# Modulation scales and shifts summed along the free axis, and a first feed-forward part that begins by pairs of feature tiles

## The chip, the cores and the metric

The kernel runs on one core of one Trainium2 chip. The core has a matrix engine (TensorE), a vector engine (VectorE), an activation engine (ScalarE), a general engine (GpSimd) and a queue engine (SyncE), each with a queue of its own that it works off in order, and transfers that are issued from SyncE's and ScalarE's queues. The metric is the time of one execution on the device in microseconds, the median of several runs. In the profile the engines are called PE (products), PEld (the weight loads of products), DVE, ACT, POOL and SP.

## The reference

Two stacks of two layers each work on 256 tokens of 1024 features, one sequence, in f32. The change concerns the first stack. There a vector `c` of 1024 features gives nine vectors of 1024 values for each layer, which scale, shift and gate the three parts of the layer:

```python
cond = jax.nn.silu(c)
for l in range(DEPTH):                                   # 2 layers
    mod = cond @ ada_w[l] + ada_b[l]                     # 1024 x 9216
    sh1, sc1, g1, sh2, sc2, g2, sh3, sc3, g3 = jnp.split(mod, N_MOD, axis=-1)

    hn = _modulate(_rms_norm(h, norm_g[l, 0]), sh1, sc1)             # xn * (1 + sc) + sh
    h = h + 0.5 * g1[:, None, :] * _swiglu(hn, ffn1_w_in[l], ffn1_w_out[l])   # 1024 -> 2 x 2816 -> 1024

    hn = _modulate(_rms_norm(h, norm_g[l, 1]), sh2, sc2)
    ...                                                  # mixing: differential and forgetting attention,
    h = h + g2[:, None, :] * (mixed @ w_out[l])          # a causal convolution, a gated spatial mixing

    hn = _modulate(_rms_norm(h, norm_g[l, 2]), sh3, sc3)
    h = h + 0.5 * g3[:, None, :] * _swiglu(hn, ffn2_w_in[l], ffn2_w_out[l])
```

The second stack follows (three kinds of attention with gates, and an MLP of 4096), without modulation.

## The kernel before

All activations stay in SBUF: `h[0]` and `h[1]` hold the residual stream of the two token tiles of 128. Weights come as units of at most 128 x 1024 f32 (0.52 MB) in one long `stream`, in the order in which they are used; `fetch` issues a transfer from SyncE's queue as long as at most 8 units are raw. A unit is converted by `pump` into a high part (a cast on ScalarE to a rounded format) and a low part (a subtraction on VectorE), and then is a chunk; units marked "whole" skip this. Each product of a chunk is made of three matmuls: high by high, high by low, low by high. All tiles of 4 KB a partition come from one ring, the arena (40 places, `c` in the profile); banks of PSUM are `bank`, small results `st`, scratch `ev`.

The order of all instructions is written out when the program is traced. `Plan` keeps an estimate of the time at which each engine ends what it was given. The main stream is the products of TensorE (`gemm_in`, `gemm_out`). Between its products `tick` calls `pump`, and moves on background generators (`Background`): the urgent ones, then the first four others, each when the plan says that its inputs are ready. `wait` and `drain` do the same until a condition holds. `pump` holds a chunk's conversion back where VectorE or ScalarE is late by the plan; units of the modulation are not held back so.

Modulation: the nine vectors of a layer are in `ada_w` as eight units each, with 128 input features as partitions and 1024 output features along the row. The first scale and shift (`v` = 1 and 0 of layer 0) come by halves of the output features, four units of 2 x 512 for each half (`first_half`). The scale of these goes through TensorE, as products with one row of output (`ada_unit`, `v == 1`), and is turned into columns by 128x1 products (`ada_turn`). All other vectors are summed on VectorE: a multiply by `cond[:, kt]` for the first unit and a multiply-add for each other. The sums over the partitions come after: for scales and shifts by 8 transposes on TensorE and 2 reductions on VectorE (`ada_columns`, `ada_reduce`), for gates (`v % 3 == 2`) by a product with ones.

`Normed` makes the input of a part: squares and their sum on ScalarE, a power on GpSimd, rows scaled by it, and `to_xT`, which transposes four feature tiles at a time into a bank, applies scale and shift by feature tile on the way out (on ScalarE for the first half of the features, on VectorE for the second) and splits the result into high and low. In the first feed-forward part of layer 0 (`st["want"] == 0`) three blocks of weights (`EARLY`) run at once, each for the first half of the features, tile 0 and tile 1, and then for the second half. The stream there is: eight half units of modulation (x's tile 0 after the fourth), the chunks for the first half of the features of three blocks (x's tile 1 among them, after the twelfth fetch), the other eight half units, and the other six chunks. The remaining 54 units of the part (part 0) follow, with the 48 units of six further vectors of layer 0 spread among the units from 4 to 50. Part 1 is the mixing part of layer 0: 24 units of `w_in` (blocks 3 and 5 whole) and 8 units of `w_out` (whole). Its output product goes through the pieces in the order forgetting attention, spatial mixing, convolution, differential attention. Parts 2, 3 and 5 are further feed-forward parts with modulation units among theirs.

Nearly all instructions are issued by one helper (line 183), so the profile's groups are told apart by engine, operation and tile.

Of the kernel before, what the change touches and what calls it, by code (L numbers as in the profile page):

```python
# [70 lines left out]
class Plan:  # L71
    """An estimate of when each engine ends what it was given, in microseconds: it orders the instructions as they are traced."""
# [24 lines left out]
    def put(self, table, ap, stamp):  # L97
        """within one engine the later stamp takes the place of an earlier one"""
# [107 lines left out]
class Background:  # L206
    """Work between the products of the main stream, as generators whose steps follow once what the last one gave
    the other engines is done. The urgent ones all move on with each tick, of the rest the first few."""
# [27 lines left out]
    def idle(self):  # L236
        """nothing for the tensor engine to do: on to the next step that is due"""
# [5 lines left out]
def two_blocks(ctx: ExitStack, tc, w, out, dbg=None, stages=99):  # L243
# [9 lines left out]
    X0, X1, EARLY = 4, 12, 3  # L253
    BOTH = 0
    WHOLE = (3, 5)
    FIRST = (0, 0, 0, 0, 0, 0)
# [17 lines left out]
    # banks of PSUM: the products of the main stream keep some to themselves  # L274
# [8 lines left out]
    # the arena: chunks of weights have a part of it to themselves  # L283
# [7 lines left out]
    def ripe(*aps):  # L291
        """the other engines are done with these"""
# [49 lines left out]
    for l in range(L):  # L342
        for i in range(3):
# [4 lines left out]
            else:  # L348
                add(f"ffn{i // 2 + 1}_w_in", l, in_sizes(FFN_BLOCKS), lambda u: u < FIRST[3 * l + i])
# [14 lines left out]
    # the modulation's weights go between those of the feed-forward parts that have time for them  # L364
# [4 lines left out]
    # the first two vectors by halves of the features: the first products begin with the first half of x's  # L369
    def first_half(v, hf):  # L370
        return [(w["ada_w"][0, at * P:(at + 2048) * P].rearrange("(k p n) -> p k n", k=2, p=P)[:, :, 512 * hf:512 * hf + 512], 1024, (0, v, (hf, j)))
                for j in range(4) for at in [(v * KT + 2 * j) * 1024]]
# [19 lines left out]
    st = dict(fetch=0, conv=0, raws=0, held=0, made=0, released=0, want=0, hurry=0, hold=True)  # L392
# [6 lines left out]
    between = {}  # L399

    def fetch():
        while st["fetch"] < len(stream) and st["raws"] < NRAW and spare():
            ap, n = stream[st["fetch"]][:2]
            t = arena.take([P, 1024])
            nc.sync.dma_start(t.rearrange("p (k n) -> p k n", k=2) if len(ap.shape) == 3 else t[:, :n], ap)
# [7 lines left out]
            if st["fetch"] in between:  # L413
                between.pop(st["fetch"])()
# [6 lines left out]
    def pump(force=False, most=None, goal=None):  # L421
        while True:
# [21 lines left out]
            if st["hold"] or st["made"] - st["released"] >= NMOST or not (spare(2) or (force and ahead <= 0 and arena.free >= 2)):  # L444
                return
# [31 lines left out]
    def release(c):  # L477
        """a chunk's last product is out; its place is free with the next tick"""
# [28 lines left out]
    cond = pool.tile([P, KT], F, name="cond")  # L507
    gains = pool.tile([P, 16], F, name="gains")
# [21 lines left out]
    def rpow(src, scale):  # L530
        """(src * scale + eps) ** -0.5"""
# [13 lines left out]
    ada_acc, mod_val, mod_there = {}, {}, {}  # L545

    def ada_unit(raw, l, v, kt):
        key = (l, v)
        gate = v % 3 == 2
        if isinstance(kt, tuple):  # L550
            hf, j = kt
            if j == 0 and v == 1:
                ada_acc[key] = aux()
            elif j == 0 and hf == 0:
                ada_acc[key] = arena.take([P, D])
            a = ada_acc[key]
            for k2 in range(2):
                k, x = 2 * j + k2, raw[:, 512 * k2:512 * k2 + 512]
                c, part = cond[:, k:k + 1], a[:, 512 * hf:512 * hf + 512] if v == 0 else a[0:1]
                if v == 1:  # L560
                    # the tensor engine has nothing else to do
# [1282 lines left out]
```

## Time and profile before

| | us |
|---|---|
| median of 3 runs (1918.46 to 1919.59) | 1918.57 |
| span of the profiled execution | 1916.7 |
| TensorE busy (products) | 1886.5 |
| VectorE busy | 1308.8 |
| ScalarE busy | 966.7 |
| GpSimd busy | 17.8 |

The profile is of one execution; times in it are us from the first instruction. The busy time of TensorE counts a product until a modelled end, so a full TensorE is not one at its peak rate. 396.80 MB are moved, all but 3.4 MB of the program's by SyncE's queue. The granted clock of TensorE is 0.996 of full speed in the mean.

### The profile page before, as it was taken

The numbers are of one execution on the slowest core, as the hardware profiler recorded it, in microseconds if no ns is written. First come the engines' busy times: TensorE is split into PE (matmuls) and PEld (weight loads), VectorE is DVE, ScalarE is ACT, GpSimd is POOL, SyncE is SP. The second block draws the span as 40 slices with busy tenths as digits, with TensorE's granted clock in tenths as the row PEclk, the third lists the DMA queues.
The fourth block names the chain that finished last, engine by engine and source line by source line (L and its number), as shares of the span: only waits on it lengthen the run. The fifth ranks groups of instructions, "written<-read, shape, count | busy, mean of one in ns | idle before, by whom it ended". The sixth has DMA issues, their size and how long they took to land.

```text
span 1916.7 us, 24124 instructions
## 1 busy us (share of the span) xinstructions
PE 1886.5 (98%) x8808; PEld 1498.3 (78%) x8808; DVE 1308.8 (68%) x1995; ACT 966.7 (50%) x1492; POOL 17.8 (1%) x56
## 2 busy tenths in 40 slices
PE   7999999999999999999999999999999999999998
PEld 3888865788888887668888787888888787888886
DVE  5999788777688877865566546666654645666561
ACT  4544456544454535564454646555543645555451
POOL 0000000000000000000000000000000000000000
PEclk9999999999999999999999999999999999999999
DMA  9999763578788876436574353654574443564460
GB/s 374 341 322 371 257 216 114 209 263 283 255 287 284 313 258 208 165 102 204 198 255 169 103 160 107 211 174 156 178 249 143 141 156 100 197 197 159 145 226 33
DMA packets 112483, 396.80 MB, mean 207 GB/s; under 512 B 12262, under 2 KB 12390, under 8 KB 112364
## 3 DMA queue, kind: packets, MB, share of 16 engines
q1 hardware_dynamic: 111068, 391.88, 59.3%
q10 hardware_dynamic: 1296, 3.38, 0.5%
q8 instruction: 69, 1.13, 0.2%
q14 instruction: 50, 0.41, 0.1%
HBM read 394.16 MB, written 1.05 MB: 206 GB/s over the span
## 4 chain that ended last, share of the span: by engine, by line
PE 87%; DVE 6%; ACT 5%; DMA 1%; issue 1%; POOLq 0%; ACTq 0%; POOL 0%; DVEq 0%
PE bank L183 87%; DVE c L183 3%; ACT c L183 2%; DVE sm L183 2%; ACT sm L183 2%; ACT L175 1%; DMA c<-in_ada_w_dram 0%; DVE st L183 0%; DMA c<-in_w_out_b_dram 0%; ACT ev L183 0%; DVE ev L183 0%; DMA col<-in_cols_dram 0%; DVE h L183 0%; ACT st L183 0%; ACT dl L183 0%
## 5 line engine op out<-in xcount | busy, mean ns | idle before, releaser
L183 PE MATMUL bank<-c,c 128*128 128x512 f32 (+3 forms) x7392 | 1763.5, 396 | 8.0 <-ACT c L183 5.8
L183 PEld LDWEIGHTS bank<-c,c 128*128 128x128 f32 (+1 forms) x7392 | 1348.3, 188 | 322.0 <-issue 45.4
L183 DVE TENSOR_TENSOR c<-c,c 128x1024 fp32r<-128x1024 f32 (+3 forms) x604 | 709.3, 1197 | 234.9 <-ACT c L183 227.5
L183 ACT CAST c<-c 128x1024 fp32r<-128x1024 f32 (+1 forms) x590 | 588.7, 1036 | 112.9 <-PE bank L183 77.6
L183 DVE SCALAR_TENSOR_TENSOR c<-c,cond,c 128x1024 f32<-128x1024 f32 (+1 forms) x126 | 153.7, 1220 | 0.8 <-DMA c<-in_ada_w_dram 0.3
L183 ACT ACTIVATE ev<-bank 128x256 f32<-128x256 f32 (+1 forms) x100 | 40.2, 402 | 195.6 <-PE bank L183 195.1
L183 ACT CAST c<-bank 128x512 fp32r<-128x512 f32 (+1 forms) x100 | 55.3, 553 | 92.1 <-PE bank L183 92.1
L183 DVE TENSOR_TENSOR c<-bank,c 128x512 fp32r<-128x512 f32 (+2 forms) x108 | 69.7, 648 | 25.3 <-ACT c L183 25.2
L183 ACT ACTIVATE junk<-h 128x512 f32<-128x512 f32 x44 | 27.8, 631 | 103.4 <-DVE h L183 97.6
L183 ACT ACTIVATE ev<-bank,st 128x512 f32<-128x512 f32 x56 | 38.6, 689 | 77.6 <-PE bank L183 77.6
L183 DVE TENSOR_TENSOR ev<-ev,bank 128x256 f32<-128x256 f32 x88 | 36.7, 417 | 56.8 <-ACT ev L183 56.4
L183 PE MATMUL bank<-con,ev 128*128 128x128 f32 x432 | 72.3, 272 | 2.6 <-DVE ev L183 2.6
L183 PEld LDWEIGHTS bank<-con,ev 128*128 128x128 f32 x432 | 55.7, 139 | 24.0 <-issue 4.3
L183 ACT CAST c<-ev 128x512 fp32r<-128x512 f32 x32 | 19.8, 620 | 99.8 <-DVE ev L183 99.6
L183 ACT ACTIVATE c<-bank,st 128x512 f32<-128x512 f32 x36 | 24.8, 689 | 75.2 <-PE bank L183 69.7
L183 DVE TENSOR_TENSOR ev<-ev 128x512 f32<-128x512 f32 x32 | 22.1, 691 | 45.5 <-ACT ev L183 45.5
L183 DVE TENSOR_TENSOR ev<-bank,c 128x512 f32<-128x512 f32 x40 | 27.4, 685 | 34.7 <-PE bank L183 34.4
L183 DVE SCALAR_TENSOR_TENSOR c<-c,col,c 128x256 f32<-128x256 f32 x120 | 48.7, 476 | 0.0
L183 DVE TENSOR_TENSOR c<-ev,c 128x512 fp32r<-128x512 f32 x32 | 22.2, 692 | 30.8 <-ACT c L183 30.7
L183 DVE TENSOR_TENSOR h<-h,bank 128x512 f32<-128x512 f32 x16 | 10.9, 683 | 42.1 <-PE bank L183 42.1
L183 ACT ACTIVATE sm<-sm,st 128x128 f32<-128x128 f32 x72 | 31.8, 443 | 14.3 <-DVE st L183 14.3
L183 PEld LDWEIGHTS bank<-con,c 128*128 128x128 f32 (+1 forms) x248 | 28.9, 143 | 11.6 <-DVE c L183 3.2
(107 smaller groups left out, 703.7 us busy)
## 6 DMA issues: line engine op xcount, KB each, us to landing
c<-in_ffn_w_in_dram SPq DMA_DIRECT2D x176, 512.0 KB, 5.0
c<-in_w_in_dram SPq DMA_DIRECT2D x152, 512.0 KB, 4.2
c<-in_ada_w_dram SPq DMA_DIRECT2D x144, 512.0 KB, 5.9
c<-in_ffn_w_out_dram SPq DMA_DIRECT2D x88, 512.0 KB, 5.7
c<-in_w_up_dram SPq DMA_DIRECT2D x64, 512.0 KB, 4.3
c<-in_w_down_dram SPq DMA_DIRECT2D x64, 512.0 KB, 4.2
c<-in_w_out_dram SPq DMA_DIRECT2D x16, 512.0 KB, 4.1
c<-in_w_o_dram SPq DMA_DIRECT2D x16, 512.0 KB, 4.5
```

The costliest lines, as they stand in the source:

```text
L175: self.eng.preload_act_table_set(table)
L183: return fn(*args, **kw)
```

## The change

Scales and shifts: their weights lie transposed in memory, 128 output features as partitions and 1024 input features along the row. `cond_row` holds silu(c) in every partition. One VectorE instruction per unit multiplies the unit by `cond_row` and sums along the row into one column of the vector's tile, with `ada_b` as the initial value; after each second unit the pair of columns is finished. The transposes, the reductions, the one-row products and the turning into columns are gone. Gates are as before.

The start: a broadcast of `c` goes out from ScalarE's queue, both tiles of x and the constants are first on SyncE's queue, and both tiles' rows are scaled before the first weights are taken. The stream then comes by pairs of feature tiles: two units of scale and two of shift, then the chunk of that pair for each of three blocks, four times. `Normed` of this part works in four steps of two feature tiles, evicted on ScalarE alone; the first three blocks run pair by pair, tile 0 and then tile 1. A chunk that these blocks ask for is converted alone, not with what else is there.

The other vectors: of the six that lay in part 0, four stay (units 2 to 48), and two, the shift and scale of the third part, go among units 16 to 32 of part 1.

```diff
-    stream = first_half(1, 0) + first_half(0, 0)
-    among = {0: (modulation(0, 2, 4, 3, 5, 7, 6), 4, 50), 2: (modulation(0, 8) + modulation(1, 1, 0, 2), 10, 60),
+    stream = []
+    among = {0: (modulation(0, 2, 4, 3, 5), 2, 48), 1: (modulation(0, 7, 6), 16, 32), 2: (modulation(0, 8) + modulation(1, 1, 0, 2), 10, 60),
              3: (modulation(1, 4, 3, 5, 7, 6), 8, 60), 5: (modulation(1, 8), 12, 56)}
     for part, us in enumerate(parts):
         if part == 0:
-            blocks = [us[4 * b:4 * b + 4] for b in range(EARLY)]
-            stream += [u for b in blocks for u in b[:2]] + first_half(1, 1) + first_half(0, 1) + [u for b in blocks for u in b[2:]]
+            sc0, sh0 = modulation(0, 1), modulation(0, 0)
+            for c in range(4):
+                stream += [u for k in (2 * c, 2 * c + 1) for u in (sc0[k], sh0[k])] + [us[4 * b + c] for b in range(EARLY)]
             us = us[4 * EARLY:]
...
-            pump(force=True)
+            pump(True, goal=i + 1 if i < 4 * EARLY else None)
...
     def ada_unit(raw, l, v, kt):
         key = (l, v)
-        gate = v % 3 == 2
...
+        if v % 3 != 2:
+            t = mod_tile(l, v)
+            ve.tensor_tensor_reduce(raw, raw, cond_row, scale=1.0, scalar=K("ada_b", 72 * l + 8 * v + kt, 1), op0=OP.mult, op1=OP.add,
+                                    accum_out=t[:, kt:kt + 1])
+            if kt % 2:
+                if v % 3 == 1:
+                    a = slice(kt - 1, kt + 1)
+                    ve.scalar_tensor_tensor(t[:, a], t[:, a], 1.0, K("norm_g", 24 * l + 8 * (v // 3) + kt - 1, 2), op0=OP.add, op1=OP.mult)
+                mod_there[key].append(kt // 2)
             return True
...
-        else:
-            for hf in range(2):
-                yield from ada_columns(l, v, hf, acc)
...
-        for hf in range(2):
+        n = KT // steps
+        for step in range(steps):
+            hf = step * 2 // steps
...
-                for j in range(4):
-                    k = 4 * hf + j
-                    if (j % 2 if st["made"] < BOTH else hf):
+                for j in range(n):
+                    k = n * step + j
+                    if steps == 2 and hf:
                         ve.tensor_scalar(x[:, j], ps[:, j], A[:, k:k + 1], B[:, k:k + 1], op0=OP.mult, op1=OP.add)
                     else:
                         sc_.activation(x[:, j], ps[:, j], AF.Identity, scale=A[:, k:k + 1], bias=B[:, k:k + 1])
...
-            order = [(b, tt, part) for part in (whole[:2], whole[2:]) for tt in range(2) for b in range(EARLY)]
+            order = [(b, tt, whole[c:c + 1]) for c in whole for tt in range(2) for b in range(EARLY)]
...
-            norms.append(Normed(mods=((l, 3 * i + 1), (l, 3 * i)), keep=i == 1 or FIRST[3 * l + i] > 0))
+            norms.append(Normed(mods=((l, 3 * i + 1), (l, 3 * i)), keep=i == 1, steps=2 if norms else 4))
...
-    between[X0], between[X1] = lambda: rows_in(0), lambda: rows_in(1)
+    nc.scalar.dma_start(cond_row, w["c"].to_broadcast([P, D]))
+    plan.clock["dma"] = 2.5
+    plan.wrote(cond_row, 5.0, "dma")
+    for tt in range(2):
+        rows_in(tt)
+    sc_.activation(cond_row, cond_row, AF.Silu)
     sc_.activation(cond, K("c"), AF.Silu)
-    for i in range(8):
-        while st["conv"] <= i:
-            pump(True, i + 1)
-        plan.clock["pe"] = max(plan.now, plan.clock["dve"] - 2.0)
-        bg.tick()
...
+    begin(lambda: all(norms[0].rs[tt] is not None for tt in range(2)))
+    pump(True, 4)
+    begin(lambda: all(norms[0].there))
...
-    a["ada_w"] = each("ada_w", lambda t: np.concatenate([lay_out(t[:, v * D:(v + 1) * D]) for v in range(9)]))
+    a["c"] = g["c"].reshape(1, D)
+    a["ada_w"] = each("ada_w", lambda t: np.concatenate([lay_out(m if v % 3 == 2 else m.T) for v in range(9) for m in [t[:, v * D:(v + 1) * D]]]))
```

## Rows read from the trace of the kernel before

**Rows 1.** The page: span's busy times by engine, and tenths in 40 slices.
```profile
PE 1886.5 (98%) x8808; PEld 1498.3 (78%) x8808; DVE 1308.8 (68%) x1995; ACT 966.7 (50%) x1492; POOL 17.8 (1%) x56
...
PE   7999999999999999999999999999999999999998
```
**Rows 2.** Stretches: length, busy us (x) of PE, PEld, DVE, ACT, POOL; PEclk, DMA share, GB/s.
```profile
20.00:30.00 10.00, 7.01 (x23) 5.60 (x24) 7.62 (x10) 8.21 (x14) 0.74 (x2) 0.67 1.03 397
...
80.00:100.00 20.00, 20.00 (x93) 16.36 (x93) 19.81 (x21) 10.15 (x14) 0.00 (x0) 1.00 0.95 324
...
260.00:280.00 20.00, 20.00 (x78) 11.92 (x75) 19.68 (x42) 5.91 (x12) 0.00 (x0) 1.00 0.63 221
280.00:300.00 20.00, 20.00 (x122) 15.37 (x121) 17.98 (x78) 13.79 (x43) 0.00 (x0) 1.00 0.47 161
300.00:320.00 20.00, 18.99 (x91) 11.08 (x90) 16.46 (x68) 15.01 (x44) 0.00 (x0) 1.00 0.32 107
320.00:340.00 20.00, 19.74 (x54) 9.21 (x53) 12.17 (x16) 11.88 (x21) 0.74 (x2) 1.00 0.25 79
```
**Rows 3.** Timeline of the start: start us, us, engine, operation, xcount [idle before <-releaser].
```profile
11.23 0.63 ACT L183 ACTIVATE junk<-h 128x512 f32<-128x512 f32 x1 [5.49 <-DMA h<-in_x_dram]
...
22.99 8.16 PE L183 MATMUL bank<-c,c 128*128 128x512 f32 x27 [3.23 <-ACT c L183]
...
31.09 7.03 PE L183 MATMUL bank<-c,cond 128*1 128x512 f32 x16
...
45.91 12.32 PE L183 MATMUL bank<-c,c 128*128 128x512 f32 x51
```
**Rows 4.** Timeline of TensorE alone, from 64 us.
```profile
64.21 4.38 PE L183 MATMUL bank<-c,c 128*128 128x512 f32 x18
...
68.56 5.74 PE L183 MATMUL bank<-c,c 128*128 128x512 f32 x24
```
**Rows 5.** Timeline of the start: eight transposes of a modulation vector.
```profile
38.05 1.09 PE L183 MATMUL bank<-con,c 128*128 128x128 f32 x8
```
**Rows 6.** Groups by form: xcount, busy us, mean ns of one, idle before, releasers.
```profile
L183 DVE TENSOR_TENSOR c<-c,c 128x1024 fp32r<-128x1024 f32 x574 | 688.4, 1221 | 228.2 <-ACT c L183 221.4 <-PE bank L183 2.2 <-DMA c<-in_ffn_w_in_dram 1.0
L183 ACT CAST c<-c 128x1024 fp32r<-128x1024 f32 x574 | 579.3, 1047 | 104.2 <-PE bank L183 77.6 <-DVE c L183 21.4 <-DMA c<-in_ffn_w_in_dram 2.0
L183 DVE SCALAR_TENSOR_TENSOR c<-c,cond,c 128x1024 f32<-128x1024 f32 x112 | 143.2, 1278 | 0.1
...
L183 DVE TENSOR_TENSOR ev<-ev,bank 128x256 f32<-128x256 f32 x88 | 36.7, 417 | 56.8 <-ACT ev L183 56.4
...
L183 DVE TENSOR_TENSOR c<-ev,c 128x512 fp32r<-128x512 f32 x32 | 22.2, 692 | 30.8 <-ACT c L183 30.7
...
L183 DVE TENSOR_REDUCE mod<-bank 128x4 f32<-128x512 f32 x22 | 15.1, 684 | 5.1 <-PE bank L183 5.1
```
**Rows 7.** Timeline of VectorE: masked minimum with accumulator output, 128 and 256 elements.
```profile
282.31 0.28 DVE L183 CUSTOM_DVE_ANT_0 sm<-bank,con 128x128 f32<-128x128 f32 x1
...
282.51 0.42 DVE L183 CUSTOM_DVE_ANT_0 sm<-bank,con 128x256 f32<-128x256 f32 x1
282.86 0.08 DVE L183 DVE_READ_ACCUMULATOR2_ANT st<- 128x1 f32 x1
```
**Rows 8.** Timelines of VectorE and TensorE in the first mixing part.
```profile
274.63 1.22 DVE L183 TENSOR_TENSOR c<-c,c 128x1024 fp32r<-128x1024 f32 x1
...
281.90 0.48 DVE L183 TENSOR_SCALAR c<-bank,col 128x256 f32<-128x256 f32 x1 [1.88 <-ACT c L183]
...
318.24 5.85 DVE L183 TENSOR_TENSOR c<-c,c 128x1024 fp32r<-128x1024 f32 x5 [1.70 <-ACT c L183]
...
328.64 0.48 DVE L183 SCALAR_TENSOR_TENSOR c<-bank,gains,sm 128x256 f32<-128x256 f32 x1
...
329.17 7.99 PE L183 MATMUL bank<-c,c 128*128 128x512 f32 x18 [0.26 <-DVE c L183]
```
**Rows 9.** Transfers by line: xcount, KB each, median us to landing.
```profile
c<-in_norm_final_dram ACTq DMA_DIRECT2D x1, 512.0 KB, 3.3
```

More of the change, by code (lines that the diff above doesn't have):

```diff
@@ L443, in pump @@
                 continue
-            if st["hold"] or st["made"] - st["released"] >= NMOST or not (spare(2) or (force and ahead <= 0 and arena.free >= 2)):
+            if st["made"] - st["released"] >= NMOST or not (spare(2) or (force and ahead <= 0 and arena.free >= 2)):
                 return
@@ L548, in ada_unit @@
         key = (l, v)
-        gate = v % 3 == 2
[L550 to L560, printed above, removed]
-                    pe.matmul(part, c, x, start=k == 0, stop=k == KT - 1)
-                elif k == 0:
-                    ve.tensor_scalar(part, x, c, None, op0=OP.mult)
-                else:
-                    ve.scalar_tensor_tensor(part, x, c, part, op0=OP.mult, op1=OP.add)
-            if j == 3:
-                bg.add((ada_turn if v == 1 else ada_columns)(l, v, hf, a), urgent=True, due=plan.ready(raw if v == 1 else a))
+        if v % 3 != 2:
[7 more added lines that the diff above has]
+                mod_there[key].append(kt // 2)
             return True
@@ L585, in ada_unit @@
         if kt == KT - 1:
[L586 to L588 removed]
+            ve.tensor_tensor(acc[0:1], acc[0:1], br[0:1], op=OP.add)
+            arena.put()
             bg.add(ada_reduce(l, v, acc), urgent=True, due=plan.ready(acc) + 2.0)
         return True
[L592 to L624 removed]
     def mod_tile(l, v):
@@ L709, in chain @@
                 rows = arena.take([P, D])
-                if st["hold"]:
-                    sc_.activation(rows, h[tt], AF.Copy, scale=self.rs[tt])
-                else:
-                    ve.tensor_scalar(rows, h[tt], self.rs[tt], None, op0=OP.mult)
+                ve.tensor_scalar(rows, h[tt], self.rs[tt], None, op0=OP.mult)
             else:
@@ L716, in chain @@
             yield
-            by = (lambda hf: all(hf in mod_there.get(m, ()) for m in self.mods) and (tt == 0 or st["made"] >= 3),
-                  lambda: [mod_val[m] for m in self.mods]) if self.mods else None
+            by = (lambda pair: all(pair in mod_there.get(m, ()) for m in self.mods), lambda: [mod_val[m] for m in self.mods]) if self.mods else None
             yield from until(lambda: room(3 if self.keep else 2))
@@ L722, in chain @@
                 self.x[tt] = arena.take([P, KT, P])
-            yield from to_xT(rows, self.gain, self.xT[tt], by, self.x[tt], there=self.there[tt], have=lambda hf: self.halves[tt] > hf)
+            yield from to_xT(rows, self.gain, self.xT[tt], by, self.x[tt], there=self.there[tt], have=lambda hf: self.halves[tt] > hf, steps=self.steps)
             if self.mods:
@@ L728, in chain, with finish @@
             st["hurry"] -= 1
-        def finish(self, tt, half):
-            wait(lambda: len(self.there[tt]) > half, "rows")
+        def finish(self, tt, pair):
+            wait(lambda: len(self.there[tt]) > pair * self.steps // 4, "rows")
         def free(self):
@@ L765, in start, with to_xT @@
                 (nc.sync, nc.scalar)[hf].dma_start(out[tt * P:tt * P + P, s], h[tt][:, s])
-    def to_xT(src, A, dst, mods=None, whole=None, there=None, have=lambda hf: True):
+    def to_xT(src, A, dst, mods=None, whole=None, there=None, have=lambda hf: True, steps=2):
         hi, lo = dst
@@ L780, in turn, with modulated @@
                 pe.transpose(banks[-1][:, j], src[:, P * k:P * k + P], ident)
+        def modulated(step):
+            return mods is None or all(mods[0](p) for p in range(4 * step // steps, 4 * (step + 1) // steps))
         yield from turn()
@@ L784, in to_xT @@
         if mods:
-            if not mods[0](0):
+            if steps == 2 and not modulated(0):
                 yield from turn()
-                yield from until(lambda: mods[0](0))
+            yield from until(lambda: modulated(0))
             A, B = mods[1]()
-        for hf in range(2):
+        n = KT // steps
+        for step in range(steps):
+            hf = step * 2 // steps
             if hf == len(banks):
                 yield from turn()
-            yield from until(lambda: (mods is None or mods[0](hf)) and (A is None or whole is not None or evr.has(1)))
-            ps, a = banks[hf], slice(4 * hf, 4 * hf + 4)
+            yield from until(lambda: modulated(step) and (A is None or whole is not None or evr.has(1)))
+            a = slice(n * step, n * step + n)
+            ps = banks[hf][:, a.start - 4 * hf:a.stop - 4 * hf]
             if A is None:
```

123 lines of the change are left out of this document (37 added, 86 removed).

## The prediction

> **What bounds the kernel now.** I read the busy times of the page first: TensorE is busy for 1886.5 of 1916.7 us, VectorE for two thirds, and after the first slice nearly every slice of TensorE shows a 9 [rows 1]. So TensorE is the bound nearly everywhere, and an edit pays where it takes instructions off TensorE or fills a stretch in which TensorE waits. Then I read single stretches in the table of stretches [rows 2]: from 80 to 100 us TensorE is full, with VectorE at 19.81 of 20 beside it, so VectorE is a second bound close behind the first in the first feed-forward part. From 260 to 320 us, in the mixing part, VectorE is at 19.68, 17.98 and 16.46 of 20, and in the next 20 us at 12.17.
>
> The start is the only long wait of TensorE. The timeline of the start [rows 3] shows the first main product at 22.99 us, a run of one-row products for the modulation at 31.09 (7.03 us), and an unbroken run of main products only from 45.91. The first three blocks hold 3 x 4 x 2 x 6 = 144 main products. Eight rows of main products, of which four are shown [rows 3, 4], count 27, 9, 12, 51, 12, 12, 18 and 24: 48 are out by 45.9, 141 by 68.56, and the 144th ends at about 69.3. From 64.21 to 68.56 there are 18 main products and 2 transposes [rows 4]; less 0.2 for the transposes (below) a main product costs 0.23 us. 144 cost 33 us, so the first 69.3 us lose 36.
>
> **The change part by part.** The execution shown spans 1916.7 us; the median of the runs is 1918.57, so 1.9 us lie around the span. I add to the span and put the 1.9 back at the end.
>
> *Transposes removed.* Of the twelve scale and shift vectors all but the first scale were summed over the partitions by 8 transposes each. Eight transposes of that form take 1.09 us from first start to last end [rows 5]; less the tail of the last one that is 0.11 each. Outside the start there are ten such vectors: four in part 0 (32 transposes, 3.5 us) and six of layer 1 (48 transposes, 5.3 us). All lie in feed-forward parts where TensorE is full, so they come off the path: -8.8 us. Two reductions a vector (0.68 us each [rows 6]) come off VectorE.
>
> *The new instruction.* A unit's product with the row of silu(c), and its sum, is now one VectorE instruction with two f32 sources in SBUF and an accumulator output. No row has that form. Nearest are the scaled sum that it replaces, two SBUF sources of the same 128x1024 (1278 ns), the subtraction (1221) [rows 6], and the masked minimum with accumulator output: of two in a row the second starts 0.20 us after the first for 128 elements, and 0.35 us are gone for 256, with the read of the accumulator (0.08) inside that [rows 7]. Carried on to 1024 elements that is 1.15 to 1.25; I take 1.2, the middle. A vector is then 9.6 us, against 0.7 + 7 x 1.2 + 2 x 0.68 + 0.4 of small ones = 10.9 before, so VectorE gains a little on every vector but the first scale, which TensorE did before and which now costs VectorE 9.6.
>
> *The start.* Ahead of all weights now go both halves of x, the constants, and a broadcast of c (0.52 MB) on ScalarE's queue; a broadcast of this shape landed 3.3 us after its issue late in the kernel [rows 9]. Transfers run at 397 GB/s [rows 2], 1.3 us for a unit. The first half of x, after 2.95 MB, was there at 11.23 [rows 3], so a landing is at about 3.8 us plus bytes over rate. In the new order the last of the sixteen modulation units lands at about 41.7 and the last of the twelve early chunks at 45.6. If transfers set the end, a cast, a subtraction and 24 products follow (1.05 + 1.15 + 5.5 [rows 4, 6]): 53.3. But VectorE gets 16 x 1.2 for the modulation, 12 x 1.15 for the low parts, 8 low parts of x of about 0.36 (half of the 0.69 for twice the size [rows 6]), 1.5 for the scaled rows and 1.6 for small ones: 39 us. Its first use is near 13 us, because the squares of x stand behind silu of the broadcast on ScalarE, and the first modulation unit stands behind both scaled rows on VectorE. Without a pause it is done at 52 and TensorE at 57.5; with 1.5 us lost at each of four pairs of feature tiles, to the evictions on ScalarE between a pair's sums and its low part, at 63.5. Bounds 53.3 and 64. I take 61.5, nearer to VectorE's end, because its load alone exceeds that of the transfers. Against 69.3 that is -8 us (-16 to -5).
>
> *Part 0 after the start.* Extras fall from 48 to 32 over 46 weight units. VectorE per unit: 1.15 + 0.7 x 1.2 + 0.4 for the hidden rows (two products of 0.42 and a subtraction of 0.69 for four units [rows 6]) = 2.4 us, against TensorE's 12 x 0.23 = 2.8. VectorE comes out of the start with hardly a chunk of lead and meets six evictions at once there: a stall of 0 to 3 us, I take +1, nearer to none since each unit gives back 0.4. The transfers, 1.7 units of 1.3 us a chunk, stay below 2.8.
>
> *Part 1.* Sixteen units move to the second half of the mixing part's weights, from unit 16 on. Their place in VectorE's queue follows the conversion of the last split chunks (the very last at 274.63 [rows 8]); from there they are taken as fast as they land. That is 16 x 1.2 = 19.2 us in a stretch where VectorE is nearly back to back up to 313 [rows 2], with one wait of 1.88 us [rows 8] and 0.3 elsewhere. Queued behind them are the masks and scalings of the differential attention, and TensorE waits for its last piece: the product at 329.17 starts after 0.26 us of idle time that VectorE ended, whose last scaling began at 328.64 [rows 8]. Upper bound: 19.2 - 2.2 of idle time = 17 us. Lower bound 0: VectorE has 7.8 us free from 320 to 340 [rows 2], and the conversions for part 2 before that, five of them in one run of 5.85 us [rows 8], can go behind. I take the middle, +9. A gain is excluded here, since nothing is removed from this stretch. What hides these units is that slack; without it they cost 17.
>
> Sum: -8 - 3.5 - 5.3 + 1 + 9 = -6.8; span 1909.9, time **1911.8 us**.
>
> **The rivals.** (a) *The slack of part 1 takes the moved units whole.* For: TensorE hardly waits there, 0.26 us in the row. Against: VectorE at 19.68 and 17.98 of 20 just ahead. Then -8 - 8.8 + 1 + 0 to 3 gives 1903 to 1906.
>
> (b) *VectorE's queue in part 1 becomes the bound* (the other side): the differential attention ends 17 us later and TensorE waits ahead of the last output products. With the start at its poor end: -5 - 8.8 + 3 + 17 = +6, 1925. It decides from the point where the moved units cost over 13 us. For: the back-to-back stretch. Against: the room from 320 on [rows 2].
>
> (c) *The start gains nothing*: VectorE's 39 us and its pauses end where the old order did. Then 0 - 8.8 + 1 + 9 gives 1920. This is also the case in which the pairs do not do what they say.
>
> [...]
>
> **How the numbers follow.** Forecast (1907 to 1917) 0.45; (a) 0.17; (b) 0.14; (c) 0.13; (d) 0.06; 0.05 for what I have not seen. A measurement of this kernel can tell about 0.2%, 3.8 us, from no change. Faster by more: (a) and the part of the forecast below 1914.7, 0.39 of its 0.45: 0.56. Within: the rest of the forecast, (c), and some of (b): 0.25. Slower: the rest, 0.19. The range from 1902 to 1925 takes in the forecast, (a), (c) and most of (b).
>
> **What would show it.** Right: the accumulating instruction at 1.2 us; no one-row products; the 144th main product ending near 61; VectorE nearly full from 13 to 55 us; 80 fewer transposes outside the start; and in the first mixing part VectorE back to back for longer, with a wait of TensorE for VectorE of about 9 us ahead of the last output products. [...] What would undo the forecast most easily is the order in which the written-out plan puts the moved units between the steps of the attention, which the trace of before cannot show.

## The result and the profile after

| | before | after |
|---|---|---|
| median of the runs, us | 1918.53 (1918.46 to 1919.59) | 1931.77 (1931.21 to 1934.03) |
| span of the profiled execution, us | 1916.7 | 1929.3 |

The change makes the kernel slower by 13.2 us: the ratio is 1.0068, with a 95% interval from 1.0054 to 1.0082. The forecast was 1911.8, with a range up to 1925.

To see where the time went I numbered the main products, TensorE's instructions of the form 128x512 from `c` tiles. There are 7008 in each trace, so the start of the n-th can be set against that of the n-th before. After stands at -2.1 us at the 144th (end of the first three blocks), -5.0 at the 792nd (end of part 0), +19.4 at the 1100th (part 1 is over) and +12.9 at the last. So the start gave 2.1 us, part 0 2.9, part 1 took 24.4, and the rest gave 6.5.

The page of after, busy times, against [rows 1]:

```profile
PE 1871.3 (97%) x8672; PEld 1491.6 (77%) x8672; DVE 1307.2 (68%) x2055; ACT 969.6 (50%) x1501; POOL 17.0 (1%) x56
```

TensorE is busy for 15.2 us less in a span 12.6 us longer: over the whole span the time is in its waits, which grow by 27.8 us. The table of stretches of after, against [rows 2] (columns as there):

```profile
40.00:60.00 20.00, 16.83 (x60) 12.83 (x59) 15.52 (x26) 11.35 (x19) 0.00 (x0) 0.83 1.03 408
80.00:100.00 20.00, 20.00 (x93) 16.42 (x92) 19.96 (x22) 10.44 (x14) 0.00 (x0) 1.00 0.84 298
260.00:280.00 20.00, 20.00 (x73) 12.43 (x72) 19.93 (x41) 5.91 (x12) 0.00 (x0) 1.00 0.89 318
280.00:300.00 20.00, 14.12 (x73) 12.08 (x71) 19.93 (x54) 7.77 (x26) 0.00 (x0) 0.97 0.99 396
300.00:320.00 20.00, 16.13 (x67) 9.70 (x68) 19.02 (x70) 6.43 (x22) 0.00 (x0) 0.69 0.23 76
```

From 260 to 320 VectorE is now at 19.93, 19.93 and 19.02 of 20 (before 19.68, 17.98 and 16.46), and TensorE falls to 14.12 and 16.13 from 280 on (before 20.00 and 18.99). The timeline of TensorE in part 1 of after, against the one in [rows 8]:

```profile
301.62 1.65 PE L183 MATMUL bank<-c 32*128 32x256 f32 x6 [7.49 <-DVE c L183]
303.19 1.54 PE L183 MATMUL bank<-con,sm 128*128 128x128 f32 x6
...
311.65 1.71 PE L183 MATMUL bank<-sm,c 128*64 128x256 f32 x8 [2.11 <-DVE sm L183]
...
329.45 0.82 PE L183 MATMUL bank<-con,sm 128*128 128x128 f32 x6
...
348.54 7.99 PE L183 MATMUL bank<-c,c 128*128 128x512 f32 x18 [1.20 <-DVE c L183]
```

The last row is the product that the prediction watched (at 329.17 before): it is 19.4 us later, but its own wait is 1.20 us. The large wait, 7.49 us for VectorE, comes 47 us earlier, ahead of the scores. What VectorE does before that, from its timeline of after:

```profile
294.29 1.28 DVE L183 CUSTOM_DVE_ANT_0 c<-c,cond_row,col 128x1024 f32<-128x1024 f32 x1
295.50 0.09 DVE L183 DVE_READ_ACCUMULATOR2_ANT mod<- 128x1 f32 x1
295.50 3.25 DVE L183 SCALAR_TENSOR_TENSOR c<-c,col,c 128x256 f32<-128x256 f32 x8
298.67 1.28 DVE L183 CUSTOM_DVE_ANT_0 c<-c,cond_row,col 128x1024 f32<-128x1024 f32 x1
299.88 0.08 DVE L183 DVE_READ_ACCUMULATOR2_ANT mod<- 128x1 f32 x1
299.88 1.28 DVE L183 CUSTOM_DVE_ANT_0 c<-c,cond_row,col 128x1024 f32<-128x1024 f32 x1
301.08 0.08 DVE L183 DVE_READ_ACCUMULATOR2_ANT mod<- 128x1 f32 x1
301.08 0.48 DVE L183 TENSOR_SCALAR c<-bank,col 128x256 f32<-128x256 f32 x1
```

The scaling at 301.08, which TensorE waits for, stands behind sums at 294.29, 298.67 and 299.88 and a run of convolution taps, without idle time. All sixteen moved sums lie between 248.94 and 302.63. The group of the new instruction by form (xcount, busy us, mean ns):

```profile
L183 DVE CUSTOM_DVE_ANT_0 c<-c,cond_row,col 128x1024 f32<-128x1024 f32 x96 | 121.9, 1279 | 0.0
```

The waits are not the whole of part 1. These rows (columns as in [rows 2]) show part 1 as one stretch, first in before, then in after, and then the three pieces of it in which after has the lower granted clock:

```profile
227.10:357.00 129.90, 126.81 (x578) 87.04 (x578) 100.75 (x262) 77.68 (x175) 2.40 (x9) 1.00 0.45 152
222.10:376.30 154.20, 135.74 (x577) 91.95 (x576) 120.67 (x298) 77.72 (x174) 2.45 (x9) 0.94 0.51 185
247.60:251.00 3.40, 3.14 (x7) 2.48 (x8) 3.40 (x7) 0.77 (x2) 0.00 (x0) 0.50 0.56 224
298.80:309.00 10.20, 7.38 (x32) 5.20 (x34) 10.10 (x34) 0.96 (x2) 0.00 (x0) 0.50 0.21 76
312.50:315.80 3.30, 3.30 (x10) 1.52 (x8) 3.27 (x13) 1.60 (x4) 0.00 (x0) 0.50 0.38 124
```

From the 792nd to the 1100th main product TensorE has 576 instructions in both kernels. In after it is idle for 18.5 us in place of 3.1, and busy for 8.9 us longer. So about 15.4 us of the loss are waits and 8.9 are the same products taking longer. For 13.8 us of its work (3.14 + 7.38 + 3.30) the clock is at 0.50; at that level a product takes about twice as long (the transposes above: 1.54 us against 0.82), so by estimate some 7 of the 8.9 us are the clock.

### The profile page after: what moved, and what is told of

Its sections match the earlier page's. It is cut to its first block, busy times and chain, and to the rows that moved or that the text cites. A ratio compares the mean times of both kernels' runs of the same rounds, so it can differ in the third digit from the quotient of the medians.

```text
span 1929.3 us, 23834 instructions
## 1 busy us (share of the span) xinstructions
PE 1871.3 (97%) x8672; PEld 1491.6 (77%) x8672; DVE 1307.2 (68%) x2055; ACT 969.6 (50%) x1501; POOL 17.0 (1%) x56
## 4 chain that ended last, share of the span: by engine, by line
PE 85%; DVE 7%; ACT 5%; DMA 2%; issue 1%; POOLq 0%; SPq 0%; POOL 0%; DVEq 0%; ACTq 0%
PE bank L183 85%; DVE c L183 5%; ACT c L183 2%; ACT sm L183 2%; DMA c<-in_ffn_w_in_dram 2%; DVE sm L183 1%; ACT L175 1%; DVE st L183 0%; DMA c<-in_w_out_b_dram 0%; ACT ev L183 0%; DVE ev L183 0%; DMA col<-in_cols_dram 0%; DVE h L183 0%; ACT dl L183 0%; ACT st L183 0%
## 5 line engine op out<-in xcount | busy, mean ns | idle before, releaser
L183 PE MATMUL bank<-c,c 128*128 128x512 f32 (+3 forms) x7392 | 1764.4, 397 | 19.7 <-ACT c L183 15.0
L183 DVE CUSTOM_DVE_ANT_0 c<-c,cond_row,col 128x1024 f32<-128x1024 f32 x96 | 121.9, 1279 | 0.0
L183 DVE TENSOR_TENSOR c<-bank,c 128x512 fp32r<-128x512 f32 (+2 forms) x108 | 69.9, 649 | 24.4 <-ACT c L183 24.1
L183 ACT CAST c<-ev 128x512 fp32r<-128x512 f32 (+1 forms) x36 | 20.6, 573 | 91.6 <-DVE ev L183 91.2
L183 DVE SCALAR_TENSOR_TENSOR c<-c,cond,c 128x1024 f32<-128x1024 f32 x42 | 53.8, 1280 | 0.0
L183 DVE TENSOR_TENSOR ev<-ev 128x512 f32<-128x512 f32 x32 | 22.1, 691 | 45.5 <-ACT ev L183 45.5
L183 DVE TENSOR_TENSOR c<-ev,c 128x512 fp32r<-128x512 f32 (+1 forms) x36 | 22.8, 633 | 29.8 <-ACT c L183 29.7
L183 DVE TENSOR_TENSOR h<-h,bank 128x512 f32<-128x512 f32 x16 | 10.9, 683 | 42.1 <-PE bank L183 42.1
```

Source lines behind the costliest of these rows:

```text
L183: return fn(*args, **kw)
```

## The experiments

Theory: the sixteen sums delay the attention because they take VectorE's time in a stretch without slack. Rivals: transfers and ring places of the moved units, or the new start. For each kernel the table gives the median, the ratio to before on the same chip with its 95% interval, and the difference from before (us, from the profiled execution) at the start of a main product. A column less the one before it is a stage: 792nd to 1100th is part 1.

| kernel | us | ratio | 144th | 792nd | 960th | 1020th | 1100th | last |
|---|---|---|---|---|---|---|---|---|
| after | 1931.77 | 1.0068 (1.0054 to 1.0082) | -2.1 | -5.0 | -6.3 | +19.4 | +19.4 | +12.9 |
| e1_all_part0 | 1912.38 | 0.9962 (0.9947 to 0.9976) | -0.2 | -3.5 | -4.9 | -0.3 | -0.2 | -5.1 |
| e2_one_moved | 1922.14 | 1.0010 (1.0000 to 1.0020) | -0.6 | -3.0 | -1.2 | +11.5 | +11.5 | +4.8 |
| e3_no_sums | 1914.30 | 0.9972 (0.9961 to 0.9984) | -2.2 | -5.0 | -2.7 | +1.1 | +1.2 | -3.8 |
| e4_before_moved | 1943.39 | 1.0122 (1.0107 to 1.0137) | +0.9 | -0.7 | -3.4 | +26.0 | +26.1 | +25.9 |
| e5_old_start | 1918.94 | 0.9989 (0.9981 to 0.9998) | +2.8 | +0.1 | -1.3 | +5.3 | +5.3 | +0.5 |
| e7_by_threes | 1913.26 | 0.9963 (0.9950 to 0.9975) | -2.0 | -4.9 | -6.3 | +0.2 | +0.4 | -4.6 |
| e8_half_sums | 1903.91 | 0.9918 (0.9904 to 0.9931) | -9.6 | -13.0 | -14.4 | -9.8 | -9.7 | -14.6 |
| e9_order | 1919.31 | 0.9995 (0.9986 to 1.0004) | 0.0 | +0.1 | +0.6 | +0.6 | +0.6 | +0.6 |
| e10_casts_first | 1905.75 | 0.9926 (0.9911 to 0.9941) | -7.7 | -10.9 | -12.3 | -7.7 | -7.7 | -12.5 |
| e11_hold | 1911.42 | 0.9959 (0.9947 to 0.9972) | -1.9 | -4.9 | -6.3 | -5.0 | -2.1 | -7.1 |
| e13_hold_gmlp | 1908.70 | 0.9947 (0.9934 to 0.9959) | -1.8 | -4.8 | -6.2 | -3.3 | -3.0 | -8.1 |
| e14_casts_hold | 1904.08 | 0.9918 (0.9903 to 0.9932) | -7.6 | -10.8 | -12.1 | -9.2 | -8.9 | -13.9 |
| e15_moved_hold | 1928.39 | 1.0054 (1.0037 to 1.0072) | -2.2 | -5.1 | -7.8 | +14.6 | +14.6 | +8.1 |
| e16_moved_early | 1935.11 | 1.0084 (1.0069 to 1.0099) | -2.2 | -5.1 | +6.4 | +22.1 | +22.1 | +15.7 |

### What the move costs

**All six in part 0**, one line of after:

```diff
-    among = {0: (modulation(0, 2, 4, 3, 5), 2, 48), 1: (modulation(0, 7, 6), 16, 32), ...
+    among = {0: (modulation(0, 2, 4, 3, 5, 7, 6), 4, 50), ...
```

> The changed kernel with all six further vectors of layer 0 in part 0 (units 4 to 50) and none in part 1. Theory A (the sixteen moved units delay the mixing part): the 25.7 us that part 1 loses between its 960th and 1020th main product are gone; part 0 gets 48 units in place of 32 and may lose 0 to 6 us, since VectorE then needs about 2.8 us a unit there, as much as TensorE. Time 1906 to 1912. Theory B (the delay of part 1 comes from the new start, which changes what is in the arena and in the queues ahead of it, and not from the move): part 1 still loses 15 us or more, time 1925 or above.

The kernel becomes faster than before by 8.3 us. Part 1 takes 3.3 us in place of 24.4, so the move is the cause and not the start. And part 0 lost nothing by taking all 48 units: it gives 3.3 us here, against 2.9 with 32. A full VectorE alone is therefore no sign of a bound: from 80 to 100 us, in part 0 of after, it is at 19.96 of 20, as full as in part 1, and TensorE is at 20.00 beside it.

**One vector moved**: `0: (modulation(0, 2, 4, 3, 5, 7), 2, 48), 1: (modulation(0, 6), 16, 32)`.

> The changed kernel with one vector (8 units) in part 1 instead of two; the other is in part 0. If the delay is VectorE's time, unit by unit, it halves: 8 x 1.2 = 9.6 us less up to 2.2 of idle time, at the ratio of the two moved vectors (25.7 us for 16 units) 13 us: time 1917 to 1922. If it is a matter of one wait that is missed (a step of the attention that slips behind a conversion, or the weight of the output that comes late), it stays near 25 us (1930) or vanishes (1907).

Part 1 takes 14.5 us, between 3.3 with none and 24.4 with two: about 10 to 11 us for each vector of 9.6 us of VectorE. It is no single missed wait.

**Transfers without sums**:

```diff
+            if l == 0 and v in (6, 7):
+                gp.tensor_copy(t[:, kt:kt + 1], raw[:, 0:1])
+            else:
                 ve.tensor_tensor_reduce(...)
```

> The changed kernel in which the sixteen moved units are transferred and take their places in the ring as before, but their sums on VectorE are left out (a copy of one column on GpSimd stands for each; the shift and scale of the third part of layer 0 are not computed). Theory A (VectorE's time): the loss of part 1 is gone but for a few us, time 1905 to 1910. Theory C (transfers and places in the arena: 8.4 MB more in the mixing part): the loss stays, 1925 or above.

Part 1 takes 6.2 us, so the sums alone are worth 24.4 - 6.2 = 18.2, and the transfers and places are not the cause of these. Part 1 of e3_no_sums as one stretch:

```profile
222.10:358.10 136.00, 129.10 (x577) 88.29 (x576) 102.06 (x267) 76.97 (x173) 11.41 (x25) 0.99 0.59 209
```

Against after, TensorE is idle for 11.6 us less and busy for 6.6 us less: nearly two thirds of the 18.2 us are waits, the rest is products that take longer. The 6.2 us that stay are 2.9 above e1_all_part0; what the transfers and places have in these was not separated.

**Before, with the two vectors moved**: the same line of the stream in the kernel before.

> The kernel before with only the two vectors moved, in the old form (multiply-add on VectorE, then transposes). Theory A: the placement alone costs 20 to 28 us in part 1, and part 0 gives back 0 to 3 because VectorE is nearly full there: time 1936 to 1946. If the placement is harmless without the new instruction or the new start, 1917 to 1922.

Part 1 takes 26.8 us. The placement alone does the harm, in the old form more than in the new one.

**The two vectors at the beginning of part 1**: `1: (modulation(0, 7, 6), 0, 16)`.

> The changed kernel with its two moved vectors among units 0 to 16 of part 1 instead of 16 to 32. VectorE is idle for 6.4 of the 20 us from 240 to 260 in the kernel before and 0.3 of the next 20. If it is the place (VectorE's back-to-back stretch of the attention) that costs, the sums fit partly into that idle time: loss of part 1 of 10 to 18 us, time 1917 to 1925. If VectorE's work is a fixed total up to the end of the part, whatever its place: 24 us or more, 1930.

The waits of TensorE by what it waited for, from 225 to 355 us (us in total, times, longest):

```profile
PE bank L183 <- ACT c L183: 10.8, 4, 4.6
PE bank L183 <- DVE c L183: 7.4, 7, 1.8
PE bank L183 <- DVE st L183: 2.8, 2, 1.7
```

Part 1 takes 27.2 us. The theory of the place, with 10 to 18 us, falls; the number of the other theory came, 24 us or more (VectorE's work as a fixed total up to the end of the part), with a time above its 1930. Of the 27.2 us, 11.2 (from -5.1 to +6.1 at the 840th product) go right at the beginning of the part, where TensorE waits for casts of its chunks, and the attention still loses 15.7 between the 960th and the 1020th. Neither end of the part has room for two vectors, although VectorE in before is idle for 6.4 us from 240 to 260.

### What part 1 takes even without the move

The kernels with the new sums lose 3.2 to 6.2 us in part 1 although nothing, or no VectorE time, was moved into it. Up to 2 us of that is the clock: e1_all_part0 and e7_by_threes give TensorE the same instructions in the same order up to the 1020th product, but from the 960th on the first loses 4.6 us at a granted clock of 1.00, and the second 6.5, with 6.8 us at 0.50. The timeline of VectorE in e1_all_part0:

```profile
303.59 1.23 DVE L183 TENSOR_TENSOR c<-c,c 128x1024 fp32r<-128x1024 f32 x1 [1.89 <-ACT c L183]
...
311.14 1.23 DVE L183 TENSOR_TENSOR c<-c,c 128x1024 fp32r<-128x1024 f32 x1 [1.40 <-ACT c L183]
...
316.80 1.23 DVE L183 TENSOR_TENSOR c<-c,c 128x1024 fp32r<-128x1024 f32 x1 [1.39 <-ACT c L183]
```

These are conversions for part 2, given out between the steps of the attention; each waits for its cast with the next step behind it. In before the first of them is at 314.06. Two runs ask whether the sums or merely the order brings them.

**Sums in the new form, old start.** The kernel before with the new instruction for all scales and shifts outside the start; the row of `c` is loaded after the start's units:

```diff
+        if not gate:
+            t = mod_tile(l, v)
+            ...
+            ve.tensor_tensor_reduce(raw, raw, cond_row, ...)
+            if kt % 4 == 3:
+                finish_mod(l, v, kt // 4)
+            return True
```

> The kernel before, with its old start and all six vectors in part 0, but every scale and shift outside the start summed by the new instruction: the transposes and reductions alone are gone. If TensorE's transposes cost what the prediction put on them, the kernel is 8.8 us faster than before (3.5 in part 0, 5.3 in layer 1), less what the first mixing part takes back (it took 4.6 us of the 4.9 won before it in the changed kernel with all six vectors in part 0): 4 to 9 us faster than before. If they were hidden: within 1 us of before. Beside the changed kernel with all six vectors in part 0 (8.3 us faster than before): equal to it if the new start is worth nothing, 3 us or more behind it if the new start gains.

The whole is 1.6 us faster, less than expected. By stages: 2.8 us lost at the start (TensorE waits 1.9 us longer there and is at a clock of 0.50 for 10.2 us, in before for 6.8), 2.7 given in part 0, 5.2 taken by part 1 with the same three conversions (307.2, 314.8, 321.4) and 6.8 us at 0.50, 4.8 given after it. So the conversions come with the new sums, whatever the start.

**Another order, no other work**: `0: (modulation(0, 2, 4, 3, 5, 7, 6), 2, 48)` in the kernel before.

> The kernel before, with its 48 modulation units of part 0 placed from unit 2 to 48 instead of 4 to 50: no instruction is added or removed, only the written-out order is another. If the order alone moves the mixing part (the 4.6 us that it took back with all six vectors in part 0 are then such a matter of order), the time differs from before by 1 to 5 us in either direction, and the difference arises in the mixing part. If not, the time is within 1 us of before.

0.6 us in the trace, and no conversion between the steps: a shift of the units alone doesn't bring them.

**Holding them back**, on e1_all_part0:

```diff
+            if not force and st["keep"]:
+                return
             if not force and st["hurry"] and ahead >= 4:
...
         gemm_in(n_, MIX_BLOCKS, evac)
+        st["keep"] = l == 0
...
                 drain(bgs[names[kt // 2]])
+                if names[kt // 2] == "conv":
+                    st["keep"] = False
```

> The changed kernel with all six vectors in part 0; in the first mixing part no chunk of the next part is converted from the end of the input products until the convolution's piece is due. Theory M1 (the 4 to 6.6 us that the mixing part takes back, whenever the new sums are used, come from conversions for the next part that now stand between the attention's steps: three conversions at 303.6, 311.1 and 316.8 us, each with 1.4 to 1.9 us of waiting for its cast, where before has its first at 314.1): the loss between the 960th and 1020th main product goes from 4.6 to under 1.5 us, and the kernel is 3 to 5 us faster than without the hold, unless the part after it starts with too few chunks. Theory M2 (the loss is TensorE's: it is ahead and waits for a chain of the attention that takes its own time): the loss stays at 4 us or more.

> The same hold, lifted one piece earlier, when the spatial mixing's piece is due, so that the next part has more chunks at its start. Theory M1: as with the longer hold, with the loss at 1 to 3 us. Theory M2: 4 us or more, as without.

From the 960th to the 1020th product the loss is 1.3 us with the long hold and 2.9 with the shorter one, against 4.6. The waits of TensorE from 270 to 330 us, first in e1_all_part0, then in e11_hold:

```profile
PE bank L183 <- DVE c L183: 1.9, 2, 1.1
PE bank L183 <- ACT sm L183: 1.9, 2, 1.4
PE bank L183 <- ACT c L183: 1.1, 3, 0.7
```

```profile
PE bank L183 <- DVE st L183: 0.9, 1, 0.9
PE bank L183 <- DVE c L183: 0.5, 1, 0.5
PE bank L183 <- ACT c L183: 0.5, 2, 0.2
```

So the conversions are the cause of this loss. (With the clock at 1.00 all through, e8_half_sums and e10_casts_first, which have no hold, lose 4.6 us there too, and e14_casts_hold, with the shorter one, 2.9.) The long hold loses 2.9 us after the 1020th product, where TensorE waits 2.3 us for the casts and subtractions of part 2's chunks; over the part the holds leave 2.8 and 1.8 of 3.3. The medians are 7.4 and 10.2 us below before, against 8.3 without a hold, and their intervals overlap: the 3 to 5 us expected of the long hold do not show in the time.

**The change with the shorter hold**:

> The changed kernel as it is, its two vectors moved to part 1, with the hold on conversions for the next part until the spatial mixing's piece. If the loss of 25.7 us between the 960th and 1020th main product is the sums' own 19.3 us and 4 to 6 us of such conversions (five in the changed kernel's trace between 321 and 338 us, with about 2 us of waiting ahead of four of them): the loss is 19 to 22 us, and the kernel 3 to 6 us faster than the change. If the sums alone cost all of it (their 19.3 us, and TensorE at half clock after a pause): 24 us or more, within 2 us of the change.

Part 1 takes 19.7 us in place of 24.4. The median is 3.4 us below that of the change, but the two ratios to before overlap in their intervals, so this gain is seen in the trace alone. And not all of the 4.7 us is the hold's: 1.4 us lie ahead of the 960th product, where the two kernels give TensorE the same instructions in the same order, and only the clock differs (3.4 us at 0.50 in after, none here). From the 960th to the 1020th it is 22.4 us in place of 25.7, so the conversions stand for about 3.3. (The trace has a wait of about 2 us ahead of three of the five that the expectation names, not of four.) Of the 24.4 us, 18.2 go with the sums (e3_no_sums) and about 3.3 with the conversions; 2.9 are not assigned.

### What holds the start

The timelines of after for one pair of feature tiles, VectorE and then ScalarE:

```profile
41.43 1.28 DVE L183 CUSTOM_DVE_ANT_0 c<-c,cond_row,col 128x1024 f32<-128x1024 f32 x1
42.63 0.09 DVE L183 DVE_READ_ACCUMULATOR2_ANT mod<- 128x1 f32 x1
43.69 0.43 DVE L183 TENSOR_TENSOR c<-ev,c 128x256 fp32r<-128x256 f32 x1 [0.96 <-ACT c L183]
44.83 0.42 DVE L183 TENSOR_TENSOR c<-ev,c 128x256 fp32r<-128x256 f32 x1 [0.72 <-ACT c L183]
45.77 3.50 DVE L183 TENSOR_TENSOR c<-c,c 128x1024 fp32r<-128x1024 f32 x3 [0.52 <-ACT c L183]
```

```profile
41.61 0.46 ACT L183 ACTIVATE ev<-bank,mod,mod 128x128 f32<-128x128 f32 x1 [5.54 <-DVE mod L183]
...
44.70 2.94 ACT L183 CAST c<-c 128x1024 fp32r<-128x1024 f32 x3
```

ScalarE idles 5.54 us until VectorE's sums are done, then evicts, and only then casts the pair's chunks; VectorE pauses 0.96 + 0.72 + 0.52 = 2.2 us. A pair takes 11.57 us (sums begin at 26.04, 37.62 and 49.19).

**Half of the sums left out**, the same edit as in e3_no_sums for `l == 0 and v == 0`, on e1_all_part0:

> The changed kernel with all six vectors in part 0, in which the eight sums of the first shift are left out (a copy of one column on GpSimd stands for each; the first shift of layer 0 is not computed). VectorE has 9.6 us less to do before the 144th main product. If VectorE's work sets the start, the 144th product starts 7 to 10 us earlier than with the sums (59 to 62 in place of 68.9). If ScalarE's chain of evictions and casts or the transfers set it: by less than 3 us.

The 144th product starts 9.4 us earlier than in e1_all_part0, and 7.7 earlier than in e11_hold, for 9.6 us of sums: VectorE's work sets the start. (Up to part 1 e1_all_part0 and e11_hold are the same, and reach the 144th product at 68.9 and 67.2, so this column is good to some 2 us.)

**The pair's chunks by threes**, then **the casts ahead of the evictions**:

```diff
-            pump(True, goal=i + 1 if i < 4 * EARLY else None)
+            pump(True, goal=EARLY * (i // EARLY + 1) if i < 4 * EARLY else None)
...
-            by = (lambda pair: all(pair in mod_there.get(m, ()) for m in self.mods),
+            by = (lambda pair: all(pair in mod_there.get(m, ()) for m in self.mods) and
+                               (self.steps == 2 or pair == 0 or st["made"] >= EARLY * (pair + 1)),
...
```

> The changed kernel with all six vectors in part 0, and at the start the three chunks of a pair are converted when the first of them is asked for, so that their casts stand on ScalarE ahead of that chunk's products and not one by one between the evictions. Theory S1 (VectorE pauses 2.2 us a pair, because a chunk's cast stands behind evictions on ScalarE that wait for VectorE's sums): the pauses go, the 144th main product starts 6 to 9 us earlier (60 to 63 us), and the kernel is 3 to 8 us faster than with chunks one by one. Theory S2 (the start is paced by VectorE's work and the transfers): the 144th product moves by less than 2 us.

> As the start by threes, but the evictions of the second, third and fourth pair also wait, in the written order, until that pair's three chunks have been given out for conversion, so that the casts do stand ahead of the evictions on ScalarE. (In the start by threes they did not: the trace shows the three casts behind the four evictions as before, and the 144th main product at 67.2 us.) Theory S1 (the 2.2 us a pair in which VectorE waits for ScalarE are lost only because the casts come last): VectorE works through, a pair takes about 9.4 us in place of 11.57, the 144th product starts at 59 to 62 us, and the kernel is 4 to 8 us faster than the start by threes. Theory S2 (transfers pace it once VectorE does not): 9.1 us a pair at best, the same region, but with TensorE waiting for chunks. If the low parts of x, now behind three subtractions on VectorE, delay TensorE by as much as the pauses did: within 2 us of 67.

The first edit alone did not test the theory, since the evictions were still written ahead of the casts. With the second, the timeline of VectorE:

```profile
34.42 0.76 DVE L183 TENSOR_TENSOR c<-ev,c 128x256 fp32r<-128x256 f32 x2
35.09 1.28 DVE L183 CUSTOM_DVE_ANT_0 c<-c,cond_row,col 128x1024 f32<-128x1024 f32 x1
...
40.11 3.49 DVE L183 TENSOR_TENSOR c<-c,c 128x1024 fp32r<-128x1024 f32 x3
43.51 0.76 DVE L183 TENSOR_TENSOR c<-ev,c 128x256 fp32r<-128x256 f32 x2
44.19 1.28 DVE L183 CUSTOM_DVE_ANT_0 c<-c,cond_row,col 128x1024 f32<-128x1024 f32 x1
```

From the second pair on no pause is left, a pair takes 9.1 us, the 144th product starts at 61.4, and the kernel is 13.1 us faster than before.

**Both edits**, casts first and the shorter hold, all six vectors in part 0:

> The changed kernel with all six vectors in part 0, with the casts of a pair ahead of its evictions, and with the hold that is lifted at the spatial mixing's piece. If the two gains add up: 7 us at the start (13.1 us below before without the hold) and 3 us from the hold: 15 to 17 us below before, about 1902 to 1904. If the mixing part's end is set by a chain that the hold doesn't touch, 13 us below, as without the hold.

16.3 us faster than before, 1904.08: the fastest kernel here that leaves nothing out. Its interval overlaps that of e10_casts_first, so the hold's share is seen in the trace (1.9 us of part 1 in place of 3.2) but not settled by the medians.

## Why the prediction was wrong

The profiled execution by the terms of the sum:

| term | predicted | after |
|---|---|---|
| start, to the 144th product | -8 | -2.1 |
| part 0 | -3.5 + 1 | -2.9 |
| part 1 | +9 | +24.4 |
| after part 1 | -5.3 | -6.5 |
| sum | -6.8 | +12.9 |

**Part 1** is the step that failed: +9 forecast, +24.4 measured. Its mechanism (VectorE's queue, with the attention behind the sums) was right; the size was not, in three ways.

First, the choice of the middle. It counted the 7.8 us that VectorE has free from 320 to 340 [rows 2] as cover, but the attention's last scaling begins at 328.64 [rows 8], and the sums stand ahead of it. VectorE in before up to there (length, busy us; clock, DMA share, GB/s):

```profile
320.00:328.64 8.64, 6.85 (x8) 1.00 0.40 121
```

Only 1.8 of the 7.8 us lie ahead of that scaling. The nearest rows were 19.68 and 17.98 of 20, and they pointed to the upper end.

Second, the sum put TensorE's clock at nothing; the estimate above gives it some 7 us of the 24.4. The upper bound of 17, the sums' time less idle time, looks close to the 18.2 measured for the sums alone, but that is in part chance: 11.6 of the 18.2 are waits, and 6.6 are products that took longer.

Third, the conversions for part 2 "can go behind" in the lower bound; in after five of them stand between the attention's steps from 321 to 338 us, and holding them back took about 3.3 us off the loss. What the prediction named as not to be seen in the trace of before was the order of the moved units, not that of these conversions. Why the planner gives them out earlier once the sums have the new form stays open.

**The start** was mis-sized too, by 5.9 us. VectorE's load was right: 13 + 39 us and four pauses of 1.5 put its end at 58, and in after it has converted the last early chunk at about 60.8, because a pair pauses 2.2 us (2.8 us more in four pairs). The 144th product ends at 67.4, 6.6 us behind that in place of 5.5. The remaining 2 us are the choice of 61.5, below the 63.5 that the sum gave with its own pauses. e10_casts_first shows the load once more: VectorE is through the fourth pair at 53.29, where the sum gives 52 and the first pair still pauses 2.2 us. That its 144th product starts at 61.4, beside the forecast 61.5, is chance: without pauses the sum gives 57.5, and the product ends at 61.8, 8.5 us behind VectorE. The sign that was named, VectorE nearly full from 13 to 55 us, did not show: it is busy for 15.52 us of the 20 from 40 to 60 in after.

**Part 0** and **the transposes** came as worked out. Part 0 gave 2.9 (forecast 2.5), and layer 1 gives 4.8 to 5.0 in e1, e3, e5 and e7 (forecast 5.3). After has 6.5 behind part 1; the other 1.6 are the clock, which is at 0.50 for 3.4 us near 750 us in before and near 745 in e1_all_part0, and nowhere between part 1 and the last main product in after.

**The rivals.** (b), VectorE's queue, is what happened, at a higher price than its 17, and together with a part of (c): the start gained a quarter of what was forecast. The wait that (b) puts ahead of the last output products did not show: it is 1.20 us there, and the longest, 7.49, stands ahead of the scores. (a) is excluded by e1_all_part0 against after: the slack took nearly nothing. (d), 0.06 of the chances, stood for a slower new instruction. No run shows one: in after, of the sums at 298.67 and 299.88 the second starts 1.21 us after the first, and one takes 1279 ns, as long as the scaled sum of before (1278 [rows 6]) and not twice as long.

## What to carry to other kernels

Work moved into a stretch where an engine is back to back and others wait for its next steps cost its whole time here, 10 to 11 us for a vector of 9.6. Free time of that engine behind those steps (7.8 us from 320 to 340 in before) did not cover it, and the 6.4 us ahead of them did not either (e16_moved_early). The waits cost more than their length here: beside 11.6 us of waits the sums cost 6.6 us in products that took longer (after against e3_no_sums). Where the work came from, part 0, it cost nothing (part 0 gives 3.3 us in e1_all_part0, 2.9 in after), although VectorE was as full there (19.96 of 20 us): ask first whether another engine waits at the place that is relieved. And where two engines hand work to each other in every step, write what needs no answer (here the casts) ahead of what does: with it the kernel is 13.1 us faster than before, without it 7.3 (e7_by_threes) and 8.3 (e1_all_part0).

## What the runs showed of the hardware

In several stretches where TensorE waits its granted clock falls, and that adds to the wait (in part 1 of after some 7 us, by the estimate above). In after it is 0.83 from 40 to 60 us, where TensorE waits about 2.1 and 0.8 us in a pair; in e10_casts_first, where no wait there is over 0.64 us, it is 1.00. The stretch of e10_casts_first, columns as in [rows 2]:

```profile
40.00:60.00 20.00, 19.00 (x85) 15.04 (x84) 19.97 (x30) 13.79 (x23) 0.00 (x0) 1.00 1.03 408
```

In part 1 of after the clock falls within the wait of 7.49 us: it is 1.00 from 294.1 to 298.8 and 0.50 from there to 309.0. The rows of after quoted above show the level: six transposes take 1.54 us at 303.19 and 0.82 at 329.45, the one at a granted clock of 0.50 and the other at 1.00. The same waits do not always bring it. In e1_all_part0 TensorE waits 2.06 and 0.76 us ahead of products at 45.85 and 47.11, and the clock is 1.00 from 40 to 50 us (0.81 in after). After and e15_moved_hold give TensorE the same instructions up to the 968th main product, and from the 792nd to the 960th it waits 2.5 us in both; the clock is at 0.50 for 3.4 us of that in after and at 1.00 throughout in e15_moved_hold, which takes 1.4 us less.
